# Output projections in three column pieces instead of two: a decoder step on one core

## The chip, the core and the metric

The kernel runs on one core of a Trainium2 chip, as one launch. The metric is the device time in microseconds. Five engines work beside each other and meet through semaphores: TensorE (PE in the profile; its weight loads are PEld), VectorE (DVE), ScalarE (ACT), GpSimd (POOL) and SyncE (SP), the last used only to issue transfers.

## The reference

One inference step of a two-layer decoder: 1024 prompt tokens and 64 sample tokens (8 sequences of 8), model width 1024. Layer 0 mixes tokens with a short gated convolution, layer 1 with differential attention; each mixer is followed by a gated feed-forward of width 2816. Four times a sub-layer ends with a matrix product back to width 1024, a residual and a layer norm:

```
y   = (gb * conv) @ w_out                        # layer 0 mixer,  1024 -> 1024
y   = attention_heads.reshape(...) @ w_out       # layer 1 mixer,  1024 -> 1024
y   = (silu(gate) * up) @ w_out                  # feed-forward,   2816 -> 1024, both layers
x   = layernorm(ALPHA * x + y) * g + b           # after each of them
```

These four products are the output projections of the title.

## The kernel before

All products are kept near fp32 precision in three passes. A tensor is split into a high part and the rest (`split_to`, ScalarE makes the high part, VectorE the rest, lines 75 and 76), and a product is hi x hi + hi x lo + lo x hi (`passes`).

Input projections (`in_type`, line 104) load a weight tile of 128 x 128 into TensorE and stream the transposed activations `xTh`, `xTl` past it, in chunks of 364, 362 and 362 of the 1088 tokens, into one accumulator tile `pin`. The projections of queries, keys and values (line 687) load activations and stream 256 columns of weights, `psqkv`. Line 752 is the product of queries and keys.

Output projections (`out_type`, line 140) do it the other way round: a tile of activations (128 features x 128 tokens: `zh`, `zl` in the convolution, `hh`, `hl` in the feed-forwards, `xTh`, `xTl` in the attention output) is the loaded operand, and the weights `whi`, `wlo` (128 x 1024) are streamed. In a row such as `pout<-whi,hh` the streamed operand comes first. The reduction is cut in bursts: as soon as a few feature tiles are there (2, 2, 1 and 3 in the convolution, nine times 2 and then 4 in each feed-forward, 2, 2 and 4 in the attention output), TensorE runs them against all 8 prompt token tiles, and VectorE adds the accumulator `pout` to the token tile's running sum `acc` or `acq` in SBUF (`residual`: line 115, or 113 with the first burst's factor or a row sum for the norm). A burst over two tiles has 8 token tiles x 2 column halves x 2 tiles x 3 passes = 96 matmuls of 512 columns. `pout` has four buffers of 128 x 512, one PSUM bank each, in the order of the loop. The 64 sample tokens go through line 125, apart from this.

In the last burst of a sub-layer, each token tile is followed by its layer norm (`ln_prompt`): row sums of the column halves (in `lsm`) give the negative mean `nmu` (line 156), ScalarE squares and sums (`junk`, 159), GpSimd makes the inverse root (`rs_t`, `rs_r`), VectorE applies both (168 and 169), and, where another layer follows, TensorE transposes the tile (`ptr`, line 216) and it is split into `xTh` and `xTl` (218 and 219). A scheduler sets the order of instructions on each engine, except where a block is marked as manual (transfers of SP in layer 1, the projections of queries, keys and values on TensorE).

Of the kernel before, what the change touches and what calls it, by code (L numbers as in the profile page):

```python
# [9 lines left out]
F32 = mybir.dt.float32  # L10
# [4 lines left out]
ALU = mybir.AluOpType  # L15
AX = mybir.AxisListType
PSUM = bass.MemoryType.PSUM

P = 128
D = 1024  # L20
KT = D // P
NS = 64
NP = 1024
NT = NS + NP
CH = ((0, 364), (364, 362), (726, 362))
TT = (0,) + tuple(NS + P * i for i in range(NP // P))
F = 2816
# [22 lines left out]
def decoder_kernel(ctx: ExitStack, tc: tile.TileContext, i_: dict, o_: dict):  # L50
    nc = tc.nc
    PE, ACT, DVE, POOL, SP = nc.tensor, nc.scalar, nc.vector, nc.gpsimd, nc.sync
# [4 lines left out]
    sml = ctx.enter_context(tc.tile_pool(name="sml", bufs=4))  # L57
    drp = ctx.enter_context(tc.tile_pool(name="drp", bufs=1, space=bass.MemoryType.DRAM))

    ident = cst.tile([P, P], F32, name="ident")  # L60
    xTh = cst.tile([P, KT, NT], F32R, name="xTh")
    xTl = cst.tile([P, KT, NT], F32R, name="xTl")
    mhalf = cst.tile([P, 1], F32, name="mhalf")
# [46 lines left out]
    def residual(a, ps, first, s):  # L110
        if first or s is not None:
            kw = {} if s is None else {"accum_out": s}
            DVE.scalar_tensor_tensor(a, a, ALPHA if first else 1.0, ps, op0=ALU.mult, op1=ALU.add, **kw)
        else:
            DVE.tensor_tensor(a, a, ps, op=ALU.add)  # L115

    def out_type(pout, st, acts, wts, first, ln=None, at=0):
        last = len(acts) - 1

        def sample():  # L120
            ss = sml.tile([P, 1], F32, name="lsms", tag="lsms", bufs=2) if ln else None
            ps = pout.tile([P, 512], F32, name="pouts", tag="pout")
            for j, ((_, _, hs), (_, _, raw)) in enumerate(zip(acts, wts)):
                for half in range(2):
                    PE.matmul(ps[half * NS:half * NS + NS, :], hs, raw[:, half * 512:half * 512 + 512],  # L125
                              start=(j == 0), stop=(j == last), skip_group_check=True)
            residual(st["s"], ps, first, ss)
            return ln_sample(pout, st, ss, ln) if ln else iter(())

        for t in range(8):  # L130
            if t == at:
                side = sample()
            t0 = NS + t * P
            s = sml.tile([P, 2], F32, name="lsm", tag="lsm") if ln else None
            for hf in range(2):
                ps = pout.tile([P, 512], F32, name="pout", tag="pout")
                cs = slice(hf * 512, hf * 512 + 512)
                for j, ((ah, al, _), (wh, wl, _)) in enumerate(zip(acts, wts)):
                    for n, (a, b) in enumerate(passes(ah, al, wh, wl)):
                        PE.matmul(ps, a[:, t0:t0 + P], b[:, cs],  # L140
                                  start=(j == 0 and n == 0), stop=(j == last and n == 2))
                residual(st[t][:, cs], ps, first, None if s is None else s[:, hf:hf + 1])
            if ln:
                ln_prompt(st, t, s, ln)
                next(side, None)
                if t >= 2 and ln["turn"]:
                    to_xT(pout, st[t - 2], t - 2)
        if ln and ln["turn"]:
            to_xT(pout, st[6], 6)
            to_xT(pout, st[7], 7)  # L150

    def ln_prompt(st, t, s, ln):
        x = st[t]
        g, b = ln["gb"]
        nmu = sml.tile([P, 1], F32, name="nmu", tag="nmu")
        DVE.tensor_scalar(nmu, s[:, 0:1], s[:, 1:2], -1.0 / D, op0=ALU.add, op1=ALU.mult)
        junk = ln["pool"].tile([P, D], F32, name="junk", tag="gb", bufs=1)
        ss = sml.tile([P, 1], F32, name="lss", tag="lss")
        ACT.activation(junk, x, AF.Square, bias=nmu[:, 0:1], accum_out=ss)
        r = rstd_of(ss, 1.0 / D, EPS)  # L160
        if t == 7 and not ln["turn"]:
            y = st[0]
            DVE.scalar_tensor_tensor(y, x, nmu[:, 0:1], g, op0=ALU.add, op1=ALU.mult)
            for eng, cs in ((SP, slice(0, 512)), (ACT, slice(512, D))):
                DVE.scalar_tensor_tensor(y[:, cs], y[:, cs], r[:, 0:1], b[:, cs], op0=ALU.mult, op1=ALU.add)
                eng.dma_start(ln["keep"][t * P:t * P + P, cs], y[:, cs])
            return
        DVE.scalar_tensor_tensor(x, x, nmu[:, 0:1], g, op0=ALU.add, op1=ALU.mult)
        DVE.scalar_tensor_tensor(x, x, r[:, 0:1], b, op0=ALU.mult, op1=ALU.add)
        if ln["keep"] is not None:  # L170
            SP.dma_start(ln["keep"][t * P:t * P + P, :], x)
# [68 lines left out]

    xsT = cst.tile([P, KT, NS], F32, name="xsT")

    # ------------------------------------------------------------ layer 0
    with tc.tile_pool(name="accp", bufs=1) as accp, \
         ExitStack() as conv_stack, \
         tc.tile_pool(name="pout0", bufs=4, space=PSUM) as pout, \
# [2 lines left out]
        tp = conv_stack.enter_context(tc.tile_pool(name="tp", bufs=1, reuse_waits="tile"))  # L249
        st = stream(accp, "acc")  # L250

        # ---- short convolution
        taps = accp.tile([P, KT, 3], F32, name="taps")
        stT = accp.tile([P, KT, NSEQ, 2], F32, name="stT")
        cpT = accp.tile([P, KT, 2], F32, name="cpT")
# [9 lines left out]
        first = {1: (w1[1], w1[2], None)}  # L265
# [16 lines left out]
        def conv_feature(f):  # L282
            gb = tp.tile([P, NT], F32, name="gb", tag="gb", bufs=1)
            gc = tp.tile([P, NT], F32, name="gc", tag="gc", bufs=1)
            u = tp.tile([P, 80 + 2 + NP], F32, name="u", tag="u", bufs=1)
# [69 lines left out]
        POOL.dma_start(o_["conv_p"], cpT)  # L355
        POOL.dma_start(o_["conv_s"], csT)

        # ---- feed forward
        def ffn(layer, pin, pout, hp, tp, st, ln):
            def feature(f):  # L360
                sg = tp.tile([P, NT], F32, name="sg", tag="gb", bufs=1)
# [24 lines left out]
            ffn(0, pin, pout, hp, tp, st,  # L386
                norm(1, tp, accp, "f32", x2_dram, lambda x: SP.dma_start(s2_dram, x)))

    # ------------------------------------------------------------ layer 1 attention
    with tc.tile_pool(name="kvp", bufs=1, reuse_waits="tile") as kvp, \  # L390
         tc.tile_pool(name="ap", bufs=1, reuse_waits="tile") as ap, \
         tc.tile_pool(name="ap2", bufs=2, reuse_waits="tile") as ap2, \
# [8 lines left out]
            return kvp.tile(shape, dtype, name=name, tag=f"kv{next(kv_slot)}")  # L401

        w0 = [load_split(i_["wqkv"][0, kh].rearrange("p k c -> p (k c)"), eng=POOL, lo_raw=kh == 0) for kh in range(2)]
        # constants of this phase
        idb = ap2.tile([P, P], BF16, name="idb", bufs=1)
        cmask = ap2.tile([P, P], BF16, name="cmask", bufs=1)
        smask = ap.tile([P, 120], F32, name="smask")
# [36 lines left out]
            DVE.tensor_tensor(vb[..., 8:16], dst[..., 0:8], sin[..., 8:16], op=ALU.mult)  # L444
            DVE.tensor_tensor(x12, va, vb, op=ALU.add)

        # ---- sample tokens: projections folded over two partition halves, then paged attention
        vs = ap.tile([P, 512], F32, name="vs")
        qT = ap.tile([P, 4, P], F32, name="qT")
        kTs = ap.tile([P, 4, P], F32, name="kTs")  # L450
# [212 lines left out]
                next(samp, None)  # L663

        RATE3 = 0.76
        # ---- prompt projections
        with tc.manual_schedule(engines={mybir.EngineType.PE}):
            for pr in range(4):
                for ty, dst in enumerate((q_dram, o_["k_p"], o_["v_p"])):
# [6 lines left out]
                    for tg in range(2):  # L676
                        nat = ap2.tile([P, 4, 256], F32, name="nat", tag="pr", bufs=4)
                        first = pr == ty == tg == 0
                        ps = [None] * 4
                        for kh, t in [(kh, t) for kh in range(2) for t in range(4)] if first else [(None, t) for t in range(4)]:  # L680
                            t0 = TT[1 + 4 * tg + t]
                            if t % 2 == 0 and not kh:
                                ps[t] = ps[t + 1] = ps2.tile([P, 2, 512], F32, name="psqkv", tag="s2")
                            for k in range(KT) if kh is None else range(4 * kh, 4 * kh + 4):
                                cs = slice((k % 4) * 256, (k % 4) * 256 + 256)
# [18 lines left out]
                        cols = slice(pr * 256, pr * 256 + 256)  # L704
                        POOL.dma_start(dst[rows, cols].rearrange("(t p) c -> p t c", p=P), nat)

        # ---- prompt attention
        def head_load(h):
            cols = slice(h * P, h * P + P)
            out = []  # L710
# [129 lines left out]
                place(*done)  # L840
        step(200)

    # ------------------------------------------------------------ attention output, feed forward
    with tc.tile_pool(name="accq", bufs=1, reuse_waits="tile") as accp, \
         tc.tile_pool(name="hq", bufs=8, reuse_waits="tile") as hp, \
         tc.tile_pool(name="tq", bufs=2, reuse_waits="tile") as tp, \
# [6 lines left out]
        st = stream(accp, "acq")  # L853
# [102 lines left out]
```

## Time and profile before

| what | value |
|---|---|
| three runs | 2845.75, 2848.94 (median), 2851.12 us |
| profiled execution, span | 2845.2 us |
| TensorE busy | 2810.5 us, 99% of the span |
| VectorE, ScalarE, GpSimd busy | 1190.4, 704.7, 253.7 us |
| mean granted clock of TensorE | 0.998 |
| matmuls of line 140 | 2880, all of 512 columns |

The profiled execution's own time is its span, and it is a little shorter than the shortest of the three runs. A matmul's recorded duration overlaps with the next matmul's, so that durations add up to more than the time; the distance between two starts in the timeline is what a matmul costs in a row of them.

### The profile page before, as it was taken

To read this page: it belongs to the slowest core of one execution; us is meant where nothing else is said; L and a number is where in the kernel's file an instruction comes from. 1 tells how busy PE (TensorE), PEld (TensorE's weight loads), DVE (VectorE), ACT (ScalarE), POOL (GpSimd) and SP (SyncE) were. 2 spreads that over 40 slices of the span, in tenths; PEclk is the share of its full clock that TensorE was granted. 3 is DMA by queue.
4 is the path that set the end of the run, shared out by engine and by line. 5 is a ranking of instruction groups with operands and counts; after the bars stand their busy time and mean duration, and the time that the engine had idled before them with its cause. 6 is when DMAs were issued, how large, how long until landed. Compare 5 with 4: busy or idle time off the path is not lost.

```text
span 2845.2 us, 45546 instructions
## 1 busy us (share of the span) xinstructions
PE 2810.5 (99%) x19092; PEld 2474.1 (87%) x19092; DVE 1190.4 (42%) x2083; ACT 704.7 (25%) x1366; POOL 253.7 (9%) x517
## 2 busy tenths in 40 slices
PE   9999999999999999999999999999999999999998
PEld 9998989999999999879888666667799999999996
DVE  4435373333333332722222566676733333333325
ACT  3111141111111111312221455562311111111111
POOL 0000020000000000311111223231200000000002
PEclk9999999999999999999999999999999999999999
DMA  6111021111111111486777888761211111111102
GB/s 225 39 39 57 25 83 42 44 43 44 45 43 45 45 44 31 137 284 205 268 273 259 290 275 297 275 211 60 75 52 45 45 45 45 45 45 45 45 30 78
DMA packets 87456, 307.50 MB, mean 108 GB/s; under 512 B 10929, under 2 KB 11586, under 8 KB 87250
## 3 DMA queue, kind: packets, MB, share of 16 engines
q1 hardware_dynamic: 76194, 265.45, 27.7%
q0 software_dynamic: 10624, 38.35, 4.1%
q8 instruction: 150, 2.46, 0.4%
q10 hardware_dynamic: 432, 0.79, 0.1%
q14 instruction: 56, 0.46, 0.0%
HBM read 282.46 MB, written 22.09 MB: 107 GB/s over the span
## 4 chain that ended last, share of the span: by engine, by line
PE 93%; DMA 2%; DVE 1%; POOL 1%; ACT 1%; issue 1%; SPq 0%; POOLq 0%; DVEq 0%; ACTq 0%
PE pin L104 46%; PE pout L140 21%; PE psqkv L687 9%; PE psS L752 3%; PE psO L590 3%; PE pso L787 2%; PE psS L532 2%; PE pouts L125 2%; PE psaT L780 1%; PE psq L474 1%; DMA vpg<-cv 1%; PE psS L755 1%; POOL rs_t L93 1%; PE pstr L726 0%; PE ptr L216 0%
## 5 line engine op out<-in xcount | busy, mean ns | idle before, releaser
L104 PE MATMUL pin<-xTh,whi 128*128 128x362 f32 (+1 forms) x2688 | 876.0, 326 | 6.4 <-ACT xTh L75 6.4
L104 PE MATMUL pin<-xTl,whi 128*128 128x362 f32 (+1 forms) x2688 | 875.6, 326 | 0.3 <-DVE xTl L76 0.3
L104 PE MATMUL pin<-xTh,wlo 128*128 128x362 f32 (+1 forms) x2688 | 875.0, 326 | 0.0
L76 DVE TENSOR_TENSOR wlo<-raw,whi 128x1024 fp32r<-128x1024 f32 (+1 forms) x197 | 239.9, 1218 | 687.9 <-PE pin L104 400.7
L104 PEld LDWEIGHTS pin<-xTh,whi 128*128 128x128 f32 x2688 | 505.6, 188 | 7.4 <-ACT xTh L75 6.4
L104 PEld LDWEIGHTS pin<-xTl,whi 128*128 128x128 f32 x2688 | 505.6, 188 | 1.6 <-DVE xTl L76 0.7
L104 PEld LDWEIGHTS pin<-xTh,wlo 128*128 128x128 f32 x2688 | 505.6, 188 | 0.1
L75 ACT CAST whi<-raw 128x1024 fp32r<-128x1024 f32 (+1 forms) x197 | 203.8, 1045 | 729.7 <-PE pout L140 379.0
L140 PE MATMUL pout<-whi,hh 128*128 128x512 f32 x704 | 279.3, 397 | 0.0
L140 PE MATMUL pout<-whi,hl 128*128 128x512 f32 x704 | 278.6, 396 | 0.0
L140 PE MATMUL pout<-wlo,hh 128*128 128x512 f32 x704 | 278.0, 395 | 0.0
L687 PE MATMUL psqkv<-whi,xTh 128*128 128x256 f32 x768 | 222.5, 290 | 0.0
L687 PE MATMUL psqkv<-wlo,xTh 128*128 128x256 f32 x768 | 214.5, 279 | 0.0
L687 PE MATMUL psqkv<-whi,xTl 128*128 128x256 f32 x768 | 214.4, 279 | 0.0
L140 PEld LDWEIGHTS pout<-whi,hh 128*128 128x128 f32 x704 | 132.6, 188 | 45.7 <-issue 14.6
L140 PEld LDWEIGHTS pout<-whi,hl 128*128 128x128 f32 x704 | 132.7, 189 | 31.2 <-issue 1.6
L367 ACT ACTIVATE sg<-pin 128x364 f32<-128x364 f32 x132 | 62.6, 474 | 388.6 <-PE pin L104 388.6
L140 PEld LDWEIGHTS pout<-wlo,hh 128*128 128x128 f32 x704 | 132.6, 188 | 30.1
L687 PEld LDWEIGHTS psqkv<-whi,xTh 128*128 128x128 f32 x768 | 144.5, 188 | 15.6 <-issue 14.5
L372 DVE TENSOR_TENSOR hf<-pin,sg 128x364 f32<-128x364 f32 x132 | 70.4, 533 | 207.0 <-PE pin L104 207.0
L115 DVE TENSOR_TENSOR acc<-acc,pout 128x512 f32<-128x512 f32 x160 | 109.3, 687 | 93.5 <-PE pout L140 93.5
L687 PEld LDWEIGHTS psqkv<-wlo,xTh 128*128 128x128 f32 x768 | 144.7, 188 | 0.0
(216 smaller groups left out, 3236.7 us busy)
## 6 DMA issues: line engine op xcount, KB each, us to landing
kpg<-ck SPq DMA_DIRECT2D x128, 512.0 KB, 5.6
vpg<-cv SPq DMA_DIRECT2D x128, 512.0 KB, 5.0
raw<-wfi SPq DMA_DIRECT2D x88, 512.0 KB, 4.0
raw<-wfo SPq DMA_DIRECT2D x44, 512.0 KB, 3.7
raw<-wqkv POOLq DMA_DIRECT2D x24, 512.0 KB, 5.6
raws<-wqkv SPq DMA_DIRECT2D x24, 512.0 KB, 6.4
raw<-wci SPq DMA_DIRECT2D x23, 512.0 KB, 3.7
acc<-xn SPq DMA_DIRECT2D x8, 512.0 KB, 9.7
```

The costliest lines, as they stand in the source:

```text
L75: ACT.copy(hi, src)
L76: (eng or DVE).tensor_tensor(lo, src, fv(hi), op=ALU.subtract)
L104: PE.matmul(ps[:, :cw], a[:, k * P:(k + 1) * P], b[:, k, c0:c0 + cw], start=(k == 0 and n == 0), stop=(k == KT - 1 and n == 2),)
L115: DVE.tensor_tensor(a, a, ps, op=ALU.add)
L125: PE.matmul(ps[half * NS:half * NS + NS, :], hs, raw[:, half * 512:half * 512 + 512], start=(j == 0), stop=(j == last), skip_group_check=True)
L140: PE.matmul(ps, a[:, t0:t0 + P], b[:, cs], start=(j == 0 and n == 0), stop=(j == last and n == 2))
L367: ACT.activation(sg[:, c0:c0 + cw], ps, AF.Silu)
L372: DVE.tensor_tensor(hf[:, :cw], ps, sg[:, cs], op=ALU.mult)
L532: PE.matmul(ps[32 * t:32 * t + 32, n, :], qp[:, 2 * t + h2, :], kp[:, 2 * t + h2, :], start=(h2 == 0), stop=(h2 == 1), skip_group_check=True)
L590: PE.matmul(O[32 * t:32 * t + 32, :], PT[:, p, 32 * t:32 * t + 32], vp[:, 2 * t:2 * t + 2, :].rearrange("p h d -> p (h d)"), start=(p == 0 ...
L687: PE.matmul(ps[t][:, t % 2, :256], a[:, k, t0:t0 + P], b_[:, cs], start=(k == 0 and n == 0), stop=(k == KT - 1 and n == 2), skip_group_che ...
L752: PE.matmul(svs[c][:, bk, :], a[cp, i, :], b_[cp, bk * w:bk * w + w], start=(m == 0), stop=(m == 2), skip_group_check=True)
```

## The change

A token tile's 1024 output columns are computed in three pieces of 342 columns instead of two of 512. The pieces start at columns 0, 342 and 682; the last one begins two columns before the second ends, since 3 x 342 is 1026. Those two columns are computed twice and the third add skips them, so it is on 340 columns. The accumulator tile keeps its size of 128 x 512 and its four buffers. The row sums are three, so the mean takes a reduction and a multiplication where it took one operation. The rest of the diff removes comments.

```
+OC, OW = ((0, 0), (342, 0), (682, 2)), 342
...
-            s = sml.tile([P, 2], F32, name="lsm", tag="lsm") if ln else None
-            for hf in range(2):
+            s = sml.tile([P, 3], F32, name="lsm", tag="lsm") if ln else None
+            for hf, (c0, skip) in enumerate(OC):
                 ps = pout.tile([P, 512], F32, name="pout", tag="pout")
-                cs = slice(hf * 512, hf * 512 + 512)
+                cs = slice(c0, c0 + OW)
                 for j, ((ah, al, _), (wh, wl, _)) in enumerate(zip(acts, wts)):
                     for n, (a, b) in enumerate(passes(ah, al, wh, wl)):
-                        PE.matmul(ps, a[:, t0:t0 + P], b[:, cs],
+                        PE.matmul(ps[:, :OW], a[:, t0:t0 + P], b[:, cs],
                                   start=(j == 0 and n == 0), stop=(j == last and n == 2))
-                residual(st[t][:, cs], ps, first, None if s is None else s[:, hf:hf + 1])
+                residual(st[t][:, c0 + skip:c0 + OW], ps[:, skip:OW], first, None if s is None else s[:, hf:hf + 1])
...
-        DVE.tensor_scalar(nmu, s[:, 0:1], s[:, 1:2], -1.0 / D, op0=ALU.add, op1=ALU.mult)
+        DVE.tensor_reduce(nmu, s, axis=AX.X, op=ALU.add, negate=True)
+        DVE.tensor_scalar(nmu, nmu, 1.0 / D, None, op0=ALU.mult)
```

VectorE, last burst of the convolution, the fourth token tile (`acc_97`) and its norm, before:

```order
L113 SCALAR_TENSOR_TENSOR acc_97,lsm<-acc_97,pout 128x512
L169 SCALAR_TENSOR_TENSOR acc_96<-acc_96,rs_r,lnb 128x1024
L113 SCALAR_TENSOR_TENSOR acc_97,lsm<-acc_97,pout 128x512
L219 TENSOR_TENSOR xTl<-ptr,xTh 128x4x128
L156 TENSOR_SCALAR nmu<-lsm 128x1
```

The same place now, with line numbers two or three higher:

```order
L115 SCALAR_TENSOR_TENSOR acc_97,lsm<-acc_97,pout 128x342
L171 SCALAR_TENSOR_TENSOR acc_96<-acc_96,nmu,lng 128x1024
L115 SCALAR_TENSOR_TENSOR acc_97,lsm<-acc_97,pout 128x342
L172 SCALAR_TENSOR_TENSOR acc_96<-acc_96,rs_r,lnb 128x1024
L115 SCALAR_TENSOR_TENSOR acc_97,lsm<-acc_97,pout 128x340
L222 TENSOR_TENSOR xTl<-ptr,xTh 128x4x128
L158 TENSOR_REDUCE nmu<-lsm 128x1
L222 TENSOR_TENSOR xTl<-ptr,xTh 128x4x128
L159 TENSOR_SCALAR nmu<-nmu 128x1
```

Three adds stand where two stood, the previous tile's two norm operations lie between them, and the mean is two operations with a split between them.

TensorE, the same burst, from one token tile's transposes to the next. Before, 18 matmuls of 512 columns stand between them; the first rows are:

```order
L191 MATMUL pln<-lsss,pairs 128x1
L216 MATMUL ptr<-ident,acc_94 128x128 x8
L140 MATMUL pout<-whi,zh 128x512
L140 MATMUL pout<-wlo,zh 128x512
L140 MATMUL pout<-whi,zl 128x512
```

Now there are 27 of 342:

```order
L194 MATMUL pln<-lsss,pairs 128x1
L219 MATMUL ptr<-ident,acc_94 128x128 x8
L142 MATMUL pout<-whi,zh 128x342
L142 MATMUL pout<-wlo,zh 128x342
L142 MATMUL pout<-whi,zl 128x342
```

The transposes stay after the same token tile, and the order of passes within a piece is the same. Over the program line 140 had 2880 matmuls and its successor has 4320.

## Prediction

> **What bounds the kernel now.** I read the page first: the busy times, the granted clock and the chain that ended last.
>
> ```profile
> PE 2810.5 (99%) x19092; PEld 2474.1 (87%) x19092; DVE 1190.4 (42%) x2083; ACT 704.7 (25%) x1366; POOL 253.7 (9%) x517
> ...
> PEclk9999999999999999999999999999999999999999
> ...
> PE pin L104 46%; PE pout L140 21%; PE psqkv L687 9%; PE psS L752 3%; PE psO L590 3%; PE pso L787 2%; PE psS L532 2%; PE pouts L125 2%; PE psaT L780 1%; PE psq L474 1%; DMA vpg<-cv 1%; PE psS L755 1%; POOL rs_t L93 1%; PE pstr L726 0%; PE ptr L216 0%
> ```
>
> TensorE sets the time from end to end, at full granted clock, and the edited matmuls (L140) are 21% of the chain. The change moves the time only through what a matmul of 342 columns costs beside one of 512. The mean duration in the groups (396 ns for L140) is no help, since matmuls overlap; what counts is the distance from one start to the next, so I went to the timeline of TensorE. These are first and last rows of unbroken stretches: an output burst of the first feed-forward, one of the second, one of the attention output, and the last burst of the convolution.
>
> ```profile
> 388.37 0.40 PE L140 MATMUL pout<-wlo,zh 128*128 128x512 f32 x1
> ...
> 392.12 0.39 PE L140 MATMUL pout<-whi,zl 128*128 128x512 f32 x1
> ...
> 475.82 0.39 PE L140 MATMUL pout<-whi,hh 128*128 128x512 f32 x1
> ...
> 480.97 0.39 PE L140 MATMUL pout<-wlo,hh 128*128 128x512 f32 x1
> ...
> 1958.19 0.39 PE L140 MATMUL pout<-wlo,xTh 128*128 128x512 f32 x1
> ...
> 1959.82 0.40 PE L140 MATMUL pout<-whi,xTl 128*128 128x512 f32 x1
> ...
> 2209.83 0.40 PE L140 MATMUL pout<-whi,hl 128*128 128x512 f32 x1
> ...
> 2213.95 0.39 PE L140 MATMUL pout<-whi,hl 128*128 128x512 f32 x1
> ```
>
> The stretches hold 16, 22, 7 and 18 steps, so a 512-column matmul costs 234.4 ns in the convolution, 234.1 in the first feed-forward, 232.9 in the attention output and 228.9 in the second feed-forward. The same instruction has a different price by stage, which matters below. The other widths, from the same view:
>
> ```profile
> 302.23 0.32 PE L104 MATMUL pin<-xTl,whi 128*128 128x362 f32 x1
> ...
> 305.75 0.32 PE L104 MATMUL pin<-xTh,wlo 128*128 128x362 f32 x1
> 305.91 0.33 PE L104 MATMUL pin<-xTh,whi 128*128 128x364 f32 x1
> ...
> 309.74 0.33 PE L104 MATMUL pin<-xTh,wlo 128*128 128x364 f32 x1
> ...
> 1200.16 0.28 PE L687 MATMUL psqkv<-wlo,xTh 128*128 128x256 f32 x1
> ...
> 1202.96 0.28 PE L687 MATMUL psqkv<-wlo,xTh 128*128 128x256 f32 x1
> ...
> 1766.81 0.31 PE L752 MATMUL psS<-qtl,qth 64*128 64x320 f32 x1
> ...
> 1767.40 0.31 PE L752 MATMUL psS<-qth,qtl 64*128 64x320 f32 x1
> ...
> 2292.72 0.33 PE L104 MATMUL pin<-xTh,whi 128*128 128x362 f32 x1
> ...
> 2296.55 0.33 PE L104 MATMUL pin<-xTh,wlo 128*128 128x362 f32 x1
> ```
>
> Steps: 22, 23, 24, 4 and 23. So 362 columns cost 160.0 ns, 364 cost 166.5, 256 cost 116.7, 320 (on 64 rows) cost 147.5, and 362 again, in the chunk that follows an output burst, 166.5. Two columns more cost 6.5 ns, and the same shape has two prices: the cost of a matmul is its columns plus something that depends on where its operands lie or on what ran before. That something decides this case.
>
> **The change part by part.** *The matmuls.* Every (weight tile, pass, token tile) now has three matmuls of 342 in place of two of 512: 1026 columns for 1024, and three weight loads for two. The reduction tiles number 8 in the convolution, 22 in each feed-forward, 8 in the attention output; with 3 passes and 8 token tiles that is 192, 528, 192 and 528 pairs, 1440 in all, so 1440 matmuls more. No row has a 342. Its price from both sides: the smallest slope is that from 256 to the fast 362, (160.0 - 116.7)/106 = 0.408 ns per column. Lower end: 160.0 - 20 x 0.408 = 151.8 ns. Upper end: all that 512 costs beyond its columns is a price per matmul, 234.1 - 170 x 0.408 = 164.7 (159.5 from the 228.9). Between them: 320 gives 147.5 + 22 x 0.408 = 156.5, 364 gives 157.5, the slow 362 gives 158.3, and the straight line between 256 and 512, the two rows in which activations are the loaded operand and weights the streamed one as here, gives 116.7 + 86/256 x (234.1 - 116.7) = 156.1, with 155.7 for the attention output and 154.4 for the second feed-forward. I take the line, because it holds the roles of the operands and four of the five estimates lie within 4 ns of it; the lower end stays as a rival.
>
> Convolution and first feed-forward, 720 pairs: 3 x 156.1 - 2 x 234.1 = +0.1 ns, +0.1 us. Attention output, 192: 3 x 155.7 - 2 x 232.9 = +1.3 ns, +0.2 us. Second feed-forward, 528: 3 x 154.4 - 2 x 228.9 = +5.4 ns, +2.9 us. Together +3.2 us, all on the path, since TensorE is what ends last in each burst.
>
> The Trainium skill, page "TensorE: Matmul & The Clock Gate", section "Back-to-back issue gap", gives N/2.4 + 2.5 ns for a warm matmul of N columns. As an estimate from that page, three of 342 take 435.0 ns and two of 512 take 431.7, so 1440 pairs would add 4.8 us. This trace does not agree with the figures: 512 takes 228.9 to 234.4 ns here, not 215.8, and the excess is not one constant.
>
> *VectorE, hidden in most bursts.* A residual add on 512 columns becomes three, on 342, 342 and 340.
>
> ```profile
> L115 DVE TENSOR_TENSOR acc<-acc,pout 128x512 f32<-128x512 f32 x160 | 109.3, 687 | 93.5 <-PE pout L140 93.5
> L372 DVE TENSOR_TENSOR hf<-pin,sg 128x362 f32<-128x362 f32 x88 | 46.8, 532 | 77.5 <-PE pin L104 77.5
> ...
> L113 DVE SCALAR_TENSOR_TENSOR acc<-acc,pout 128x512 f32<-128x512 f32 x64 | 43.8, 684 | 23.8 <-PE pout L140 23.7
> L156 DVE TENSOR_SCALAR nmu<-lsm 128x1 f32<-128x1 f32 x32 | 6.8, 212 | 0.6
> L113 DVE DVE_READ_ACCUMULATOR acc<-acc,pout 128x1 f32 x32 | 2.6, 82 | 0.0
> ```
>
> Slope (687 - 532)/150 = 1.03 ns per column, so a 342 add takes 687 - 176 = 511 ns. A piece over two weight tiles keeps TensorE busy for 6 x 156 = 0.94 us, so VectorE waits as it does now, and the four accumulators still give it three pieces of slack: the cover is there. In the one burst over a single tile (third of the convolution) a piece is 3 x 156 = 0.47 us against 0.51: 24 x 0.04 = 1 us at most, less than the slack, taken as 0.
>
> Where a norm follows, a token tile adds 3 x 511 - 2 x 687 = 159 ns, one accumulator read (82) and one small operation for the mean (212): 0.45 us. The second feed-forward and the bursts over four tiles cover it (12 x 2 x 229 ns = 5.5 us of TensorE per tile). The last burst of the convolution has 3 tiles, 4.2 us per token tile, and there VectorE sets the pace:
>
> ```profile
> 375.42 0.68 DVE L113 SCALAR_TENSOR_TENSOR acc<-acc,pout 128x512 f32<-128x512 f32 x1
> 376.02 0.08 DVE L113 DVE_READ_ACCUMULATOR acc<-acc,pout 128x1 f32 x1
> 376.48 1.28 DVE L169 SCALAR_TENSOR_TENSOR acc<-acc,rs_r,lnb 128x1024 f32<-128x1024 f32 x1 [0.38 <-POOL rs_r L95]
> 377.69 0.68 DVE L113 SCALAR_TENSOR_TENSOR acc<-acc,pout 128x512 f32<-128x512 f32 x1
> 378.29 0.08 DVE L113 DVE_READ_ACCUMULATOR acc<-acc,pout 128x1 f32 x1
> 378.29 0.69 DVE L219 TENSOR_TENSOR xTl<-ptr,xTh 128x512 fp32r<-128x512 f32 x1
> ```
>
> Its rows follow one another almost without a gap. Ends: 0 if TensorE's slack elsewhere takes it, 8 x 0.45 = 3.6 us if every tile waits. TensorE stalls in only part of the eight tiles, so I take +1.5.
>
> *The end.* The last tile has a shorter last add (511 for 687 ns) and one small operation more (212): +0.04 us, nothing. *Nothing else moves much*: no DMA is added, SP and POOL issue the same transfers, ScalarE the same casts; the scheduler swaps a few neighbours around the norms. Each added accumulator group brings a wait of its first matmul on a free accumulator, with the rest of the piece behind it on TensorE; today such waits total:
>
> ```profile
>   DVE acq L113: 0.8, 1
>   DVE acc L113: 0.6, 2
> ```
>
> 1.4 us over 432 groups; with 648 groups they stay small as long as VectorE keeps up, and they are in the 1.5.
>
> Sum: +3.2 + 1.5 = +4.7 us. The profiled execution spans 2845.2 us, 0.6 us below the lowest of the three runs and 3.7 below their median of 2848.94: it would become 2849.9, and the median 2853.6, 0.16% up. A change under 0.2% (5.7 us) cannot be told from none here, so my forecast is no change.
>
> **The rivals.** *Fast pieces.* The fast 362 starts at a column that is no multiple of 16, while the 364 chunk starts at column 0; two of the three new pieces start at 342 and 682. If all pieces get the fast price of 151.8 ns: 3 x 151.8 - 468.2 = -12.8 ns over 720 pairs, -10.4 over 192, -2.4 over 528, in all -12.5 us; with the 1.5 the median is 2838. For it: almost all 362 chunks run at 160 ns. Against: these stream activations and not weights, and all 256 and 512 rows show more excess per column. It decides below about 154 ns a piece.
>
> *Slow pieces.* The price of the slow 362, 166.5 - 8.2 = 158.3 ns, holds: +6.7 ns over 720, +9.1 over 192, +17.1 over 528, +15.6 us; median 2866. For it: that price appears right behind output bursts and agrees with 364. Against: it is left again after one chunk pair.
>
> *A full price per matmul.* The Trainium skill, page "Perfetto Trace Analysis", section "Matmuls", says that larger matmuls are more efficient than smaller ones when possible. In the rows it would mean that the excess belongs to the instruction: 164.7, 163.5 and 159.5 ns a piece, +25.9 ns over 720, +24.7 over 192, +20.7 over 528, together +34.3 us; median 2885. Against: per column, 256, 364 and 512 cost 0.456, 0.457 and 0.457 ns, and 362 only 0.442: the rows do not rise as columns get fewer.
>
> *VectorE sets the pace in more bursts*, with adds and waits at both upper ends, 1 + 3.6 in place of 1.5: median 2855. Little speaks for it, with VectorE at 42%.
>
> **How the numbers follow.** Forecast 35% (own range 2848 to 2859), fast pieces 28%, slow pieces 27%, full price 6%, VectorE 4%. Of the forecast's 35, 24 lie within 0.2%, 10 slower, 1 faster; of the fast pieces 27 are faster, 1 the same; slow pieces and full price are slower; VectorE is split. So faster 0.28, same 0.27, slower 0.45. The predicted time is the forecast's 2853.6. The range is 2836 to 2870: it leaves out the full price and the outer edges of fast and slow pieces, some 19 in 100.
>
> **What would show it.** Steps of about 156 ns between starts in the first feed-forward's bursts, and about 154 in the second's; an unbroken burst over two tiles (96 matmuls now, 144 then) of nearly the same length in the first, and about 0.3 us longer in the second; adds near 0.51 us; the norm tail of the convolution a microsecond or two longer. Steps near 152 or 158 mean one of the rivals, and different steps by piece, that the start column decides. The forecast falls if a price appears that no width here has, or if TensorE waits for accumulators in bursts over two tiles.

## Result and profile after

The changed kernel takes 2861.36 us (median of 6 runs), the kernel before 2848.90 on the same chip (6 runs). The ratio is 1.0054, 95% interval 1.0042 to 1.0065: 12 to 19 us slower, 15.4 by the ratio (the medians differ by 12.5). It lies inside the predicted range, but the forecast of no change did not hold: +4.7 us had been summed and about three times as much came. The profiled execution spans 2861.6 us against 2845.2, +16.4, and that difference is what the traces can be asked for.

The page of the changed kernel, with its busy times and the heads of the chain that ended last:

```profile
PE 2825.4 (99%) x20532; PEld 2614.6 (91%) x20532; DVE 1220.6 (43%) x2363; ACT 706.2 (25%) x1366; POOL 256.2 (9%) x517
...
PE pin L106 46%; PE pout L142 20%; PE psqkv L690 9%; PE psS L755 3%; PE psO L593 3%; PE pso L790 2%; PE psS L535 2%; PE pouts L127 2%; PE psaT L783 1%; PE psq L477 1%; POOL rs_t L95 1%; PE pstr L729 1%; PE psS L758 1%; PE psT L582 1%; ACT junk L162 0%
```

TensorE still ends everything, with 1440 instructions more; VectorE has grown by 30 us and stays far from being the bound. The page doesn't say where 16 us went. Four landmarks do, each a first matmul of its kind (start, length in us): the first burst of the first feed-forward and that of the second, from the chain of waits, and the first matmul of the queries' projection (`psqkv`) and of the sample tokens' projection (`psq`), from the timeline of TensorE. Before:

```profile
472.28 22.68 PE pout L140 x96
...
1192.79 0.37 PE L687 MATMUL psqkv<-whi,xTh 128*128 128x256 f32 x1
...
1211.08 0.62 PE L474 MATMUL psq<-raws,xsT 128*64 128x256 f32 x2 [2.48 <-DMA raws<-wqkv]
1213.51 3.63 PE L474 MATMUL psq<-raws,xsT 128*64 128x256 f32 x14 [1.82 <-DMA raws<-wqkv]
...
2124.49 22.18 PE pout L140 x96
```

After:

```profile
473.66 22.71 PE pout L142 x144
...
1197.02 0.36 PE L690 MATMUL psqkv<-whi,xTh 128*128 128x256 f32 x1
...
1219.31 4.86 PE L477 MATMUL psq<-raws,xsT 128*64 128x256 f32 x16 [6.30 <-DVE nlam L436]
...
2134.24 22.87 PE pout L142 x144
```

| stretch | before, us | after, us | change |
|---|---|---|---|
| start to the first feed-forward's first burst | 472.3 | 473.7 | +1.4 |
| from there to the first `psqkv` | 720.5 | 723.4 | +2.9 |
| first `psqkv` to first `psq` | 18.3 | 22.3 | +4.0 |
| first `psq` to the second feed-forward's first burst | 913.4 | 914.9 | +1.5 |
| from there to the end | 720.7 | 727.4 | +6.7 |

The third row has no edited matmul at all: a quarter of the loss lies in 20 us at the turn from layer 0 to layer 1. (Before, TensorE waits a second time just behind the third row's end, for 1.8 us, as the rows show; after, it does not.)

**The steps.** First and last rows of unbroken stretches of pieces in the changed kernel: a burst of the first feed-forward (38 steps), the attention output (39) and a burst of the second feed-forward (39).

```profile
477.77 0.32 PE L142 MATMUL pout<-whi,hl 128*128 128x342 f32 x1
...
483.71 0.32 PE L142 MATMUL pout<-wlo,hh 128*128 128x342 f32 x1
...
1983.74 0.32 PE L142 MATMUL pout<-wlo,xTh 128*128 128x342 f32 x1
...
1989.91 0.32 PE L142 MATMUL pout<-wlo,xTh 128*128 128x342 f32 x1
...
2139.78 0.32 PE L142 MATMUL pout<-whi,hl 128*128 128x342 f32 x1
...
2145.92 0.32 PE L142 MATMUL pout<-whi,hl 128*128 128x342 f32 x1
```

A piece takes 156.3 ns in the first feed-forward, 158.2 in the attention output and 157.4 in the second feed-forward, where a matmul of 512 had been cheapest.

**Bursts and what follows them.** The bursts stand in the landmarks above (22.68 and 22.18 us before, 22.71 and 22.87 after). Between two of them lies an input stretch (`pin`, 288 matmuls that the change does not touch); from the chain of waits, in the first and the second feed-forward, before:

```profile
780.13 46.75 PE pin L104 x288
...
2431.10 47.06 PE pin L104 x288
```

After:

```profile
782.90 47.05 PE pin L106 x288
...
2444.28 47.06 PE pin L106 x288
```

In the first feed-forward the burst is nearly unchanged (+0.03 us) and the input stretch behind it is 0.30 us longer; nine of both make +3.0, the +2.9 of the table. In the second it is the burst, +0.69, and nine make +6.2 of the +6.7. The 0.30 has a place: the first 48 matmuls of 362 columns behind a burst, before and after, and in the changed kernel also the 362s of the second weight tile behind a later burst (47 steps each):

```profile
498.80 0.32 PE L104 MATMUL pin<-xTh,whi 128*128 128x362 f32 x1
...
506.32 0.32 PE L104 MATMUL pin<-xTh,wlo 128*128 128x362 f32 x1
```

```profile
500.21 0.33 PE L106 MATMUL pin<-xTh,whi 128*128 128x362 f32 x1
...
508.04 0.33 PE L106 MATMUL pin<-xTh,wlo 128*128 128x362 f32 x1
...
798.74 0.32 PE L106 MATMUL pin<-xTh,whi 128*128 128x362 f32 x1
...
806.26 0.32 PE L106 MATMUL pin<-xTh,wlo 128*128 128x362 f32 x1
```

160.0 ns before, 166.6 after, and 160.0 again from the second weight tile on: 48 x 6.6 ns = 0.32 us. It is the slow price of a 362 that the prediction had quoted from behind the second feed-forward's bursts; the change brought it to the first one's.

**The turn of the layers.** VectorE, last token tile's norm and the splits of layer 1's weights next to it; before:

```profile
1194.83 1.28 DVE L168 SCALAR_TENSOR_TENSOR acc<-acc,nmu,lng 128x1024 f32<-128x1024 f32 x1
1196.03 1.22 DVE L76 TENSOR_TENSOR wlo<-raw,whi 128x1024 fp32r<-128x1024 f32 x1
1197.70 1.28 DVE L169 SCALAR_TENSOR_TENSOR acc<-acc,rs_r,lnb 128x1024 f32<-128x1024 f32 x1 [0.46 <-POOL rs_r L95]
```

After:

```profile
1199.93 1.22 DVE L78 TENSOR_TENSOR wlo<-raw,whi 128x1024 fp32r<-128x1024 f32 x1
1201.06 1.28 DVE L171 SCALAR_TENSOR_TENSOR acc<-acc,nmu,lng 128x1024 f32<-128x1024 f32 x1
1202.26 1.22 DVE L78 TENSOR_TENSOR wlo<-raw,whi 128x1024 fp32r<-128x1024 f32 x1
1203.39 1.28 DVE L172 SCALAR_TENSOR_TENSOR acc<-acc,rs_r,lnb 128x1024 f32<-128x1024 f32 x1
```

A split of weights now stands ahead of each of the two norm operations instead of one between them. SP stores that tile, then issues the constants, of which the last is `lam`, then the sample projection's weights (`raws`). Before and after:

```profile
1199.02 0.33 SPq L171 DMA_DIRECT2D x_dram<-acc  x1
...
1203.51 0.67 SPq L427 DMA_DIRECT2D lam<-lam  x1
1204.23 4.42 SPq L470 DMA_DIRECT2D raws<-wqkv  x6
```

```profile
1204.70 0.33 SPq L174 DMA_DIRECT2D x_dram<-acc  x1
...
1209.22 0.35 SPq L429 DMA_DIRECT2D gs<-subg  x1
1211.06 0.33 SPq L430 DMA_DIRECT2D lam<-lam  x1
1211.43 4.97 SPq L473 DMA_DIRECT2D raws<-wqkv  x6
```

Counted from the first `psqkv`, the store leaves 6.2 us later before and 7.7 after, and the weights 11.4 and 14.4. In the chain of waits of the changed kernel the store's landing has come in:

```profile
1204.70 6.34 DMA x_dram<-acc
...
1211.90 8.54 DMA raws<-wqkv
```

`lam` is issued when that store has landed. Most of the 6.34 us pass while SP issues the other constants: only the 1.5 us from the end of `gs` to `lam` are a pause of its queue, and before the change there is none. So of the 3.0 us by which the weights leave later, half is the late norm and half this pause; they then take 1.0 us longer to let the first `psq` start. TensorE stands for 6.3 us ahead of it, where it stood for 2.5 and then 1.8 before. The row names VectorE's `nlam` as the releaser; the last experiment shows that `psq` doesn't need it.

### The profile page after: what moved, and what is told of

It reads as the page before. It is cut to its first block, busy times and chain, and to the rows that moved or that the text cites. A ratio compares the mean times of both kernels' runs of the same rounds, so it can differ in the third digit from the quotient of the medians.

```text
span 2861.6 us, 48716 instructions
## 1 busy us (share of the span) xinstructions
PE 2825.4 (99%) x20532; PEld 2614.6 (91%) x20532; DVE 1220.6 (43%) x2363; ACT 706.2 (25%) x1366; POOL 256.2 (9%) x517
## 4 chain that ended last, share of the span: by engine, by line
PE 93%; DVE 2%; DMA 2%; POOL 2%; issue 1%; ACT 1%; SPq 0%; POOLq 0%; DVEq 0%; ACTq 0%
PE pin L106 46%; PE pout L142 20%; PE psqkv L690 9%; PE psS L755 3%; PE psO L593 3%; PE pso L790 2%; PE psS L535 2%; PE pouts L127 2%; PE psaT L783 1%; PE psq L477 1%; POOL rs_t L95 1%; PE pstr L729 1%; PE psS L758 1%; PE psT L582 1%; ACT junk L162 0%
## 5 line engine op out<-in xcount | busy, mean ns | idle before, releaser
L142 PE MATMUL pout<-whi,hh 128*128 128x342 f32 x1056 | 338.4, 321 | 0.0
L142 PE MATMUL pout<-wlo,hh 128*128 128x342 f32 x1056 | 337.1, 319 | 0.0
L142 PE MATMUL pout<-whi,hl 128*128 128x342 f32 x1056 | 337.0, 319 | 0.0
L142 PEld LDWEIGHTS pout<-whi,hh 128*128 128x128 f32 x1056 | 198.5, 188 | 16.3 <-issue 14.6
L142 PEld LDWEIGHTS pout<-whi,hl 128*128 128x128 f32 x1056 | 198.6, 188 | 1.6 <-issue 1.6
L142 PEld LDWEIGHTS pout<-wlo,hh 128*128 128x128 f32 x1056 | 198.1, 188 | 0.0
L690 PEld LDWEIGHTS psqkv<-whi,xTh 128*128 128x128 f32 x768 | 144.5, 188 | 15.6 <-issue 14.5
L117 DVE TENSOR_TENSOR acc<-acc,pout 128x342 f32<-128x342 f32 (+1 forms) x240 | 121.4, 510 | 84.0 <-PE pout L142 83.6
L117 DVE TENSOR_TENSOR acq<-acq,pout 128x342 f32<-128x342 f32 (+1 forms) x216 | 110.0, 510 | 84.7 <-PE pout L142 84.6
```

The source lines that it names most:

```text
L142: PE.matmul(ps[:, :OW], a[:, t0:t0 + P], b[:, cs], start=(j == 0 and n == 0), stop=(j == last and n == 2))
L690: PE.matmul(ps[t][:, t % 2, :256], a[:, k, t0:t0 + P], b_[:, cs], start=(k == 0 and n == 0), stop=(k == KT - 1 and n == 2), skip_group_che ...
```

## Experiments

The theory after these rows: three causes add up, the dearer piece in the second feed-forward (about 7 us), the slow 362 behind the first one's bursts (about 3) and the two-operation mean with the order that it brings (about 5). The rivals: a price per matmul that both layers pay alike; scatter between executions; and, for the steps, either the width of a piece or the place of its operands as the cause. All differences below are against runs of the kernel before that were made together with the kernel in question.

### The kernel before again

No edit; it shows what differs between two profiles of one kernel.

> The kernel before, unchanged, for a second profile of it. Between the first two profiles (before and changed) the stretch from the end of layer 0's queries-keys-values start (about 1217 us) to the attention output (about 1971 us) grew by some 4 us, though it holds none of the edited matmuls but a few. If that is scatter between executions (theory), this second profile of before shows that stretch different from the first by 2 us or more. If it belongs to the change (rival), it agrees with the first within 1 us. Steps of 512-column matmuls: 234.2 ns in layer 0's feed-forward and 228.9 in layer 1's again; input stretch between two bursts 46.84 and 47.15 us again.

One run of 2844.6 us. Bursts and input stretches repeat to 0.01 us; the stretch from the first `psqkv` to the first `psq` is 17.0 instead of 18.3, and from there to the second feed-forward's first burst 912.9 instead of 913.4. So 0.3 us on an input stretch is no scatter, 1 us between the landmarks in the middle is. The scatter of 2 us or more that had been expected behind the turn did not come.

### Pieces in one layer only

```
+THREE, TWO = (((0, 0), (342, 0), (682, 2)), 342), (((0, 0), (512, 0)), 512)
+PLAN = [THREE]                      # the other kernel: [TWO]
...
+        OC, OW = PLAN[0]            # in out_type
...
+        PLAN[0] = TWO               # ahead of the attention output; the other: THREE
```

Both keep the two-operation mean in both layers. Layer 0 only:

> Three pieces in layer 0 only (convolution and first feed-forward), two halves in layer 1. Theory (the cost is local, by stage): the bursts of layer 0 cost what they did (22.6 us each), the input chunks behind each burst go to the slow price (47.14 for 46.84 us, twelve times 0.3 = 3.6 us), the norm tails add 1 to 3 us: +5 to +7 us in all. Rival 1 (the attention stage is late because layer 0 ends otherwise): +9 to +12 us. Rival 2 (nearly all belongs to the second feed-forward): +0 to +2 us.

Layer 1 only:

> Two halves in layer 0, three pieces in layer 1 (attention output and second feed-forward). Theory: nine bursts of the second feed-forward 0.69 us longer each (22.78 for 22.09), the last one 1.4, the attention output 1 to 2: +8 to +10 us, and input stretches stay at 47.15. Rival 1: +4 to +6. Rival 2: +12 to +15.

Layer 0 only: 1.0026 (1.0016 to 1.0037), +7.4 us. Layer 1 only: 1.0042 (1.0030 to 1.0054), +12. Bursts and input stretches are those of the changed kernel in the layer that has pieces and those of before in the other. The two add up to 19.4, more than the 15.4 of the whole, and layer 1 only was above what was expected: in its trace the stretch to the first `psq` is 21.5 us although layer 0 has halves. What both kernels share was counted twice, and that is the mean.

### The mean alone

```
-        DVE.tensor_scalar(nmu, s[:, 0:1], s[:, 1:2], -1.0 / D, op0=ALU.add, op1=ALU.mult)
+        DVE.tensor_reduce(nmu, s, axis=AX.X, op=ALU.add, negate=True)
+        DVE.tensor_scalar(nmu, nmu, 1.0 / D, None, op0=ALU.mult)
```

The kernel before, with halves, and this edit alone.

> The kernel before (two halves of 512 everywhere), with one part of the change alone: the mean from a reduction and a multiplication in place of one operation. Theory: in VectorE's order the second operation lets a weight split (wlo, line 76), which waits for a transfer of wqkv, slip ahead of the last token tile's first norm operation at the end of layer 0; the last tile's store comes 4 to 5 us later, SP issues the transfers of the sample projections behind it, and TensorE waits for them: stretch from the first queries-keys-values matmul to the first sample projection 21 to 22 us in place of 17 to 18; with a microsecond in the convolution's norm tail +4 to +6 us in all. Rival (two small operations of 0.2 us each are hidden, as the prediction had it): within 1 us.

1.0018 (1.0009 to 1.0027), +5.1 us, as expected in total. The bursts are as before. The turn has less of it than expected: 20.6 us from the first `psqkv` to the first `psq` instead of 21 to 22, and SP pauses for 0.7 us ahead of `lam`.

```profile
1194.89 0.37 PE L688 MATMUL psqkv<-whi,xTh 128*128 128x256 f32 x1
...
1215.52 0.62 PE L475 MATMUL psq<-raws,xsT 128*64 128x256 f32 x2 [4.13 <-DVE nlam L434]
```

The rest lies elsewhere. In this profile the stretch ahead of the first feed-forward is 474.3 us (472.3 before) and the one from the first `psq` to the second feed-forward 915.6 (913.4 and 912.9 in the two profiles of before). So 5.1 us of the loss come from one more operation on 128 numbers per token tile and the order of instructions that it brings, spread over three places. With it the account closes: layer 0 only less the mean is 2.3, layer 1 only less the mean 6.9, and 2.3 + 6.9 + 5.1 = 14.3 against 15.4 measured, within the intervals, which reach about 3 us to either side in each of these three kernels.

### The sums of two pieces combined early

```
+                if ln and hf == 1:
+                    DVE.tensor_scalar(s[:, 3:4], s[:, 0:1], s[:, 1:2], -1.0 / D, op0=ALU.add, op1=ALU.mult)
...
-        DVE.tensor_reduce(nmu, s, axis=AX.X, op=ALU.add, negate=True)
-        DVE.tensor_scalar(nmu, nmu, 1.0 / D, None, op0=ALU.mult)
+        DVE.tensor_scalar(nmu, s[:, 2:3], -1.0 / D, s[:, 3:4], op0=ALU.mult, op1=ALU.add)
```

The changed kernel with one small operation behind the last add, as before the change; the other stands a piece earlier.

> The changed kernel with the mean taken differently: the first two row sums are added and scaled before the third piece's add, and one operation after it finishes the mean. On VectorE the last tile's first norm operation then stands ahead of the weight split again, as before the change. Theory: 4 to 5 us less than the changed kernel (first queries-keys-values matmul to first sample projection 17 to 18.5 us), so +10 to +12 us against before. Rival (the delay comes from the three adds and not from the mean): the same time as the changed kernel, +15 us.

1.0063 (1.0049 to 1.0077): no gain, a miss, though 10 to 12 us above before had been expected. The norm's first operation is ahead of the weight split again, and still the store leaves 7.2 us after the first `psqkv` (rows of TensorE and of SP) and the first `psq` starts 20.4 us after it:

```profile
1198.52 0.37 PE L691 MATMUL psqkv<-whi,xTh 128*128 128x256 f32 x1
...
1205.73 0.33 SPq L175 DMA_DIRECT2D x_dram<-acc  x1
```

The order of split and norm was thus not the whole cause. What else makes the last norm late in this order, the three adds or the two small operations, was not tried by itself. What remained of the theory was the part behind the store: SP's queue. The last experiment takes that away.

### Weights of the sample projection ahead of the constants

```
+        early = []
+        for kh in range(2):
+            for half in range(2):
+                raw = kv_tile("raws", [P, 4, 256])
+                SP.dma_start(raw, i_["wqkv"][6 * half, kh])
+                early.append(raw)
+
         w0 = [load_split(...) for kh in range(2)]
```

The changed kernel; these four loads stand behind the last store and ahead of the constants, and the sample projection uses them instead of its first four.

> The changed kernel, with the first four weight loads of the sample projection issued by SP directly behind the last token tile's store, ahead of the constants and of lam, which waits until that store has landed. Matmuls, adds and the mean stay as changed. Theory (the +4 to 5 us at the end of layer 0 come from SP, which holds these loads behind the landing of a store that the norm made late): the loads leave about 6 us earlier than in the changed kernel, the first matmul of the sample projection starts 16 to 17 us after the first of the queries' projection (22.3 in the changed kernel, 17.0 to 18.3 before), and the kernel takes about 2855, that is 8 to 11 us more than before and 5 to 7 less than the changed kernel. Rival (the loads are bound by transfer rate or something else gates them, or the late constants make a new wait): the time stays at 14 to 16 us above before.

1.0029 (1.0020 to 1.0039), +8.3 us instead of +15.4, as expected. SP's queue and the first `psq`, which comes 16.0 us after the first `psqkv`, without a wait:

```profile
1204.93 3.03 SPq L410 DMA_DIRECT2D raws<-wqkv  x4
...
1217.71 0.42 SPq L437 DMA_DIRECT2D lam<-lam  x1
```

```profile
1196.84 0.36 PE L700 MATMUL psqkv<-whi,xTh 128*128 128x256 f32 x1
...
1212.79 2.56 PE L487 MATMUL psq<-raws,xsT 128*64 128x256 f32 x16
```

The norm is as late as in the changed kernel (the loads behind its store leave 8.1 us after the first `psqkv`), and TensorE no longer notices. `psq` runs before `lam` has been asked for, so `nlam` was not what it waited for. The 7 us include the wait of 4.3 that the kernel before has there too, and the edit removes SP's constants from the weights' way as well as the pause ahead of `lam`; so it shows what TensorE waited for, and not what the change added. The same edit in the kernel before was not tried.

### Where operands lie

Six kernels move an operand or cut the columns elsewhere, with the count of matmuls unchanged. The intermediate of the first feed-forward 32 bytes further, in the kernel before:

```
-                hh = hp.tile([P, NT], F32R, name="hh", tag="h")
-                hl = hp.tile([P, NT], F32R, name="hl", tag="h")
+                off = 8 if layer == 0 else 0
+                hh = hp.tile([P, NT + 16], F32R, name="hh", tag="h")[:, off:off + NT]
+                hl = hp.tile([P, NT + 16], F32R, name="hl", tag="h")[:, off:off + NT]
```

> The kernel before (two halves of 512), with one difference: the activation tiles hh and hl of the first feed-forward start 32 bytes later, so that they have the address modulo 64 bytes that the second feed-forward's have (32 in place of 0). Theory (the price of a matmul depends on where the loaded operand lies): the 512-column step of the first feed-forward falls from 234.2 to 228.9 ns, a burst from 22.59 to 22.09 us, and the input stretch behind it rises from 46.84 to 47.15; 1056 steps x 5.3 = -5.6 us, +3 us for the chunks behind, so -2 to -4 us in all. Rival (the stage, its pools or banks set the price): steps stay at 234.2 and the time within 1 us.

The same in the changed kernel, for the second feed-forward (`off = 8 if layer == 1`):

> The changed kernel, with the activation tiles hh and hl of the second feed-forward 32 bytes later, so that they start at 0 modulo 64 bytes as in the first (tiles are 4416 bytes apart in both in place of 4352). Theory (the place of the loaded operand sets the step): the 342-column step of the second feed-forward falls from 157.4 towards the first's 156.35 ns, a burst from 22.78 to 22.62 us, 0.16 x 10 = 1.6 us less than the changed kernel, +13 to +15 us against before. Rival (the second feed-forward is dearer for another reason): 22.78 stays.

The changed kernel with pieces of 352, 336 and 336 at 0, 352 and 688 (`OC = ((0, 352), (352, 336), (688, 336))`):

> The changed kernel with pieces of 352, 336 and 336 columns at 0, 352 and 688, all starts multiples of 64 bytes apart and no column twice. Theory (a piece's price is its columns plus what its place costs, about the same on average for any start): 2 columns fewer, -0.8 ns per three pieces, about -1 us against the changed kernel, so +14 us. Rival A (starts off a multiple of 64 bytes are the dear ones): 10 us or more less than the changed kernel. Rival B (they are the cheap ones, as the fast 362 chunks suggest): 4 us or more above it.

The transposed activations 24 bytes further, in the kernel before, and the same by 32 bytes (`8:8 + ...`):

```
-    xTh = cst.tile([P, KT, NT], F32R, name="xTh")
-    xTl = cst.tile([P, KT, NT], F32R, name="xTl")
+    xTh, xTl = (cst.tile([P, KT * NT + 16], F32R, name=n)[:, 6:6 + KT * NT].rearrange("p (k t) -> p k t", k=KT)
+                for n in ("xTh", "xTl"))
```

> The kernel before, with the transposed activations xTh and xTl placed 24 bytes later. The input chunks then start at 24, 8 and 48 modulo 64 bytes instead of 0, 48 and 24; widths, order and everything else are the same. Theory (place sets the price): the 364-column step falls from 166.5 to about 161 ns, 2688 steps x 5.5 = up to -15 us. Rival (the 364 chunk is dear by its width): its step stays at 166.5 and the time within 3 us. The 362 steps may go either way.

> The kernel before, with xTh and xTl 32 bytes later (24 bytes later cost 46 us). Input chunks then start at 32, 16 and 56 modulo 64 bytes, streamed operand and weights both at 32 in the first. Theory (place, not width, sets the step): the steps of 364 and 362 differ from 166.5 and 160.0 by more than 2 ns, in either direction, and the 512 step of the attention output, whose loaded operand is xTh, goes from 233.3 to 229 ns as in the second feed-forward. Rival (only shifts that are no multiple of 32 bytes matter): steps within 1 ns of those before, time within 3 us.

The kernel before with input chunks of 362, 364, 362 instead of 364, 362, 362:

> The kernel before, with input chunks of 362, 364 and 362 columns at 0, 362 and 726 in place of 364, 362 and 362: the wide chunk is now the second. Theory (place): the chunk at column 0 keeps a step near 166 ns though it has 362 columns, and the 364 chunk at 362 gets about 161; time within 2 us of before. Rival (width: a count that is a multiple of four is dear): the first chunk falls to 160 and the second rises to 166.5, time also about the same; the steps tell them apart.

Burst and input stretch (us) are rows of the chain of waits like those shown above, read from each kernel:

| kernel | against before | first FF: burst, input | second FF: burst, input |
|---|---|---|---|
| before | | 22.68, 46.75 | 22.18, 47.06 |
| after | 1.0054 | 22.71, 47.05 | 22.87, 47.06 |
| before, `hh`, `hl` +32 bytes | 1.0013 (1.0005 to 1.0022) | 22.49, 47.06 | 22.41, 47.05 |
| after, `hh`, `hl` +32 bytes | 1.0048 (1.0034 to 1.0062) | 22.81, 46.74 | 22.80, 47.06 |
| after, 352/336/336 | 1.0032 (1.0020 to 1.0044) | 22.65, 47.06 | 22.70, 46.75 |
| before, `xTh`, `xTl` +24 bytes | 1.0162 (1.0148 to 1.0176) | 22.69, 48.24 | 22.20, 48.24 |
| before, `xTh`, `xTl` +32 bytes | 1.0096 (1.0080 to 1.0111) | 22.68, 47.84 | 22.19, 47.84 |
| before, chunks swapped | 1.0098 (1.0083 to 1.0114) | 22.68, 47.84 | 22.19, 47.85 |

Few came out as expected: the shift of `hh` in the kernel before was to save 2 to 4 us and cost 3.7, the 24 bytes were to save up to 15 and cost 46, the swap was to do nothing and cost 28. The pieces of 352 and 336 columns were to stand at +14 us and stand at +9. The shift in the changed kernel met its total (+13.7 us) by other parts, since the first feed-forward's input stretch became fast again and the second's burst only 0.07 us shorter. The 32 bytes moved the steps of the 362 columns by 5 to 6 ns, as expected, but that of the 364 by less than 1 (167.1 ns), and the attention output did not get cheaper. What they do show: the same instructions take another time when an operand lies 24 or 32 bytes further. Timeline rows of the middle chunk in the kernel before and with the 24 bytes (23 steps each):

```profile
783.97 0.32 PE L104 MATMUL pin<-xTh,whi 128*128 128x362 f32 x1
...
787.65 0.32 PE L104 MATMUL pin<-xTh,wlo 128*128 128x362 f32 x1
```

```profile
798.74 0.33 PE L104 MATMUL pin<-xTh,whi 128*128 128x362 f32 x1
...
802.59 0.33 PE L104 MATMUL pin<-xTh,wlo 128*128 128x362 f32 x1
```

160.0 ns against 167.4. And place is not all. With the chunks swapped, the third chunk still has 362 columns at column 726 of the same tile, and is no longer cheap:

```profile
797.72 0.33 PE L104 MATMUL pin<-xTh,whi 128*128 128x362 f32 x1
...
801.56 0.33 PE L104 MATMUL pin<-xTh,wlo 128*128 128x362 f32 x1
```

167.0 ns where it had 160.0 to 160.4: what ran before it, or beside it, counts too. The first chunk, now of 362 columns at column 0, takes 163.5 ns and the 364 behind it 168.2, so neither the place nor the width alone gives the prices that either side had expected. The two kernels with `hh` and `hl` moved also have tiles 64 bytes longer in both feed-forwards, and the second feed-forward of the first one, not shifted, went from 22.18 to 22.41: the distance between tiles is a cause beside the offset, so these two kernels don't separate them. For the change itself the 352/336/336 cut matters: same count of matmuls, all starts and widths multiples of 16, no column twice, and 6 us less, 0.17 a burst and 0.31 an input stretch in the second feed-forward. The intervals leave 1 to 11 us for this difference; the traces give 4.3 of it to the second feed-forward. So part of the loss is a matter of where the cuts fall and how wide the pieces are; whether another cut would save more is open.

## Why the prediction was right or wrong

**First feed-forward's pieces, +0.1 us: right.** 156.3 ns against 156.1 forecast, and bursts of the same length. The line between 256 and 512 happened to hit.

**Second feed-forward's pieces, +2.9 us: the sign right, the size wrong.** The step was to lower the piece's price with that of a 512 there, to 154.4 ns. The 512 had been cheap (228.9), the piece isn't: 157.4. The missing 3.0 ns x 3 x 528 make 4.8 us, the largest part of the miss. The cheapness went with how the operands lie, since it shrank when the tiles of that stage lay 64 bytes further apart (22.41 us a burst for 22.18), and it did not carry over to another width.

**Attention output, +0.2 us: too small.** 158.2 ns for 155.7, so 192 x (3 x 158.2 - 2 x 232.9) = +1.7 us. The stretch that holds it grew by 1.5, but that is no evidence for it: it grew by as much or more in two kernels with halves there (915.6 us with the mean alone and 915.7 with pieces in layer 0 only, against 914.9).

**The rival of slow pieces** had 158.3 ns everywhere and +15.6 us, and the time came out near its 2866, mostly by chance. Its mechanism did not happen in the 720 pairs of the convolution and the first feed-forward; the second feed-forward came near it.

**No term for the input stretches: wrong.** The prediction said that the slow 362 appears right behind output bursts and used it as a price for a piece. It did not ask whether the change would bring it behind the bursts that had none. It did: 0.30 us on each of nine input stretches of the first feed-forward, about 3 us there.

**VectorE and the tails, +1.5 us (0 to 3.6): about right where it was placed.** Adds of 342 take 511 ns as forecast:

```profile
L117 DVE TENSOR_TENSOR acc<-acc,pout 128x342 f32<-128x342 f32 (+1 forms) x240 | 121.4, 510 | 84.0 <-PE pout L142 83.6
```

That row is the mean over adds of 342 and 340 columns. The stretch with the convolution's tail grew by 1.4 us, but not shown by the adds: with halves and the new mean alone it grew by 2.0. (The rival that VectorE sets the pace is off by its own terms: 1 + 3.6 in place of 1.5 gives 2856.7, not 2855.)

**"Nothing else moves much": wrong, and the step that hid a quarter to a third of the loss.** It was argued from what is issued: the same transfers, the same casts. But the last norm of layer 0 has a reader behind it: its store, then a queue in which the next layer's first weights stand behind the constants and, when the store is late, behind its landing. The mean alone costs 5.1 us, and with the weights ahead of the constants the changed kernel is 7 us faster. The prediction's own fence of VectorE's order was at the convolution's last burst; it did not look at the other norm of layer 0, behind which TensorE runs only 120 `psqkv` matmuls before it needs these weights.

**Signs named beforehand.** 156 ns in the first bursts came, 154 in the second did not; a burst 0.3 us longer there was 0.69. A price far from all widths' did not appear, nor did waits for accumulators, the two signs that were to bring the forecast down: waits of output matmuls put down to adds with a row sum total 1.3 us after the change (1.4 before), and two more, 1.1 us, are put down to the mean's second operation. The larger wait that appeared was for a DMA.

**Open.** No rule was found that gives a step from addresses, widths and what ran before; how the 5.1 us of the mean divide between the convolution's tail, the turn of the layers and the attention behind it is only read from the profiles, not tried by itself, and why the attention has a share was not found.

## What to carry to other kernels

Price a new matmul shape from a row with the same operands at the same place, not from the mean of its stage, and keep a range of some 5% where there is none (362 columns took 160.0 to 167.4 ns here); look also at what the untouched matmuls behind it will do. When an engine with much idle time gets even one small operation more in a norm, follow its result to the end of the stage: to the store, to the queue that issues it, and to what stands in that queue behind it. Loads that the next stage begins with belong ahead of constants that are needed later and of a wait for the store's landing; here that move gave back 7 us, about as much as the dearer pieces of the second feed-forward cost.

## What the hardware showed beyond the prediction

A matmul of 362 columns in a dense row of them took 160.0 to 167.4 ns and one of 512 took 228.9 to 234.4, at a granted clock of 1.00 in the stretches read and without a wait, by the place of its operands and by what ran before or beside it. Moving two constant tiles by 24 bytes, with no other edit, made the kernel 1.6% slower (1.0148 to 1.0176), three times what the whole change did. The slow price came on 48 untouched matmuls behind a burst, 6.6 ns each, and not on the next weight tile's. Where `xTh` and `xTl` had not moved and the chunks kept their order, a chunk of 362 took 160.0 to 160.4 ns a step or 166.5 to 166.8, and nothing between: in the eight input stretches read from four kernels, a change in the burst ahead switched it from one to the other.
